# A one-layer streaming encoder: the finale of the last token block of the second feed-forward, turned by diagonal gate matrices behind the last down-projection

## The chip, the cores and the metric

The kernel runs on one core of a Trainium2 chip. The metric is the device time of one execution in microseconds. A run is timed three times and the median counts. The profile is one further execution, with its own time.

Engines are named as in the profile: PE is TensorE (PEld its weight loads), DVE is VectorE, ACT is ScalarE, POOL is GpSimd, SP is SyncE, which here issues every DMA of the program.

## The reference

One layer, cut to what this change touches. It runs for a prompt of 1024 tokens and a sample of 32 tokens, with `D_MODEL` 1024 and `D_FF` 2816; prompt and sample have their own conditioning vector `c`, and so their own gate `g3`.

```python
    x = x + g2[:, None] * rmsnorm(o, gains[3])
    h = adaln_in(x, gains[4], sh3, sc3)
    x = x + FFN_RES * g3[:, None] * rmsnorm(swiglu(h, w2_gate, w2_up, w2_down), gains[5])
    return x, rows
```

`swiglu(h) = (silu(h @ w_gate) * (h @ w_up)) @ w_down`; `rmsnorm` divides each token by the root of its mean square over the 1024 features and multiplies by a gain per feature. All inputs and outputs are float32.

## The kernel before, in words

The 1056 tokens (prompt, then sample) are worked in three blocks `TB`: 0 and 1 have 384 tokens, block 2 has 256 prompt tokens and the 32 of the sample. Activations lie with features on the partitions: a block is `[128, 8, w]`, eight slices `k` of 128 features by `w` tokens. The products of the feed-forward are three float32r matmuls each (`mm3`, L325 to L327).

The second feed-forward is `ffn("h3", ...)`. It goes over 22 slices of `D_FF` in groups of two. For each block, `up` makes gate and up products of both slices (PSUM tiles `gate`, `up`, from the pool of three one-bank buffers, `p1`), ACT and DVE make the gated activation, and `down` multiplies it with the rows of `w_down`: four steps `mp` of 12 matmuls, each into a two-bank tile `dn` (pool `p2`, two buffers), which DVE adds to the accumulator `facc` (L581). In the last group `down(0)` runs behind the first `up` of block 1, `down(1)` behind the first `up` of block 2, and `down(2)` at the very end.

Beside the matmuls runs a list of generators, `side`; `step` advances one of them, `finish` drains the list. Two kinds matter here:

- `tokens_first(tb)` loads the residual stream of a block (`raw`, from `xs`) and turns it by 128x128 transposes on PE (`px`, L1293) to tokens on the partitions; ACT copies the results to `xp` (L1294).
- `finale(tb)` begins in step with the last `down` of its block. `sumsq` squares two slices at a time on ACT (L364), adds them on POOL or DVE (L368, L370) and sums over the features by matmuls with a column of ones (`pss`, L357); `rstd_cols` and `rsqrt` make one reciprocal root per token, 10 small DVE operations in a chain (`rv`, `ry`, `rt`, L334 to L391). Meanwhile every slice of `facc` is multiplied by the gate coefficient of its features (`gcoef`, L1304 on ACT, L1306 on DVE). Then each 128-token tile is transposed in two halves of four slices (`py`, L1313, a `p1` buffer each), and DVE computes `xp = py * rstd + xp` (L1315). One DMA per token tile writes the output (L1318). A block has three token tiles; the third of block 2 is the 32-token sample.

The program is written in this order, and the tile framework's scheduler orders each engine's instructions from it; on the chip each engine works through its list in that order. When the last down-projection was written, `finish` had been called only for block 0, so block 1's finale and block 2's `tokens_first` are drained by the steps of `down(2)` and behind it.

Of the kernel before, what the change touches and what calls it, by code (L numbers as in the profile page):

```python
# [17 lines left out]
KT = D // 128  # L18
# [56 lines left out]
def encoder_step(ctx: ExitStack, tc, x_prompt, x_sample, cache_a_k, cache_a_v, cache_b_k, cache_b_v,  # L75
# [33 lines left out]
    def p2(name, shape=(128, 2, 512)):  # L109
        return ps2.tile(list(shape), F32, name=name, tag="p2")  # L110
# [231 lines left out]
    def token_cols(w):  # L342
        return [(c, min(128, w - c)) for c in range(0, w, 128)]

    def sumsq(src, kts, w, bank, ends, fold=True):


        n = len(kts) // 2
        pss = bank("pss")
        cols = token_cols(w)  # L350
        behind = []

        def add_up(sq, first, last):
            halves = (0,) if fold else (0, 1)
            for q in halves:
                for j, (c0, m) in enumerate(cols):
                    te.matmul(pss[:m, j:j + 1], sq[:, q, c0:c0 + m], ones, start=first and j == 0 and q == 0,  # L357
                              stop=last and q == halves[-1], skip_group_check=True)

        acc, first = None, True  # L360
        for c in range(n):
            k = kts[2 * c]
            sq = h_tile([128, 2, 384], "sq")
            ae.activation(sq[:, :, :w], src[:, k:k + 2, :w], AF.Square)  # L364
            if fold:
                e = SQE[c % len(SQE)]
                e = ve if e == "v" else ge
                e.tensor_tensor(sq[:, 0, :w], sq[:, 0, :w], sq[:, 1, :w], op=OP.add)  # L368
                if acc is not None:
                    e.tensor_tensor(sq[:, 0, :w], sq[:, 0, :w], acc[:, 0, :w], op=OP.add)  # L370
                acc = sq
            if behind:
                add_up(*behind.pop())
            if c in ends or not fold:
                behind.append((sq, first, c == n - 1))
                acc, first = None, False
            yield
        add_up(*behind.pop())
        return pss

# [96 lines left out]
    def step(n):  # L477
        for _ in range(n):
            while side:
                turn[0] += 1  # L480
                i = turn[0] % min(ABREAST, len(side))
                try:
                    next(side[i])
                    break
                except StopIteration:
                    side.pop(i)

    def finish():
        while side:
            step(1)  # L490
# [3 lines left out]
    def begin(key, gen, first=False):  # L494
        side.insert(0 if first else len(side), marked(key, gen))
# [29 lines left out]
    def ffn(key, H, F, wg, wu, wd, per_group, key_out, after, beside=lambda ff, tb: None):  # L525
        late, pre = [], {}
        plan = rounds(*ROUNDS[key])
        begun = set()
        final = {tb: max(i for i, (g, t) in enumerate(plan) if tb in t) for tb in range(3)}

        def load(r, ff):
            pre[r, ff] = (split_cols(wg, ff), split_cols(wu, ff))

        load(0, 0)
        yield
        for r, (gi, blocks) in enumerate(plan):
            grp = GROUPS[gi]
            wgu, wds, gs = {}, {}, {}

            def up(ff, tb):  # L540
                need((key, tb))
                w = TB[tb][1]
                hi, lo = H[tb]
                ps = [p1("gate"), p1("up")]
                for s in range(2):
                    for k in range(KT):
                        mm3(ps[s][:, :w], wgu[ff][s], k, hi[:, k, :], lo[:, k, :], k == 0, k == KT - 1)
                    step(FAST if gi == 0 else PACE)
                sl = s_tile([128, 384], "sl")
                ae.activation(sl[:, :w], ps[0][:, :w], AF.Silu)  # L550
                ve.tensor_tensor(sl[:, :w], sl[:, :w], ps[1][:, :w], op=OP.mult)  # L551
                g = g_tile([128, 2, 384], "gg", F32R)
                ae.activation(g[:, 0, :w], sl[:, :w], AF.Copy)
                ve.tensor_sub(g[:, 1, :w], sl[:, :w], g[:, 0, :w])  # L554
                gs[ff, tb] = g
                beside(ff, tb)
                if late:
                    late.pop()()

            def down(tb, r=r, grp=grp, wds=wds, gs=gs):  # L560
                w = TB[tb][1]
                new = tb not in begun
                begun.add(tb)
                if new:
                    F[tb] = u_tile(tb, "facc", F32)
                if r == final[tb]:
                    if key_out != "y" or tb == 0:
                        finish()
                    own = marked((key_out, tb), after(tb))
                for mp in range(KT // 2):  # L570
                    ps = p2("dn")
                    for s in range(2):
                        for i, ff in enumerate(grp):
                            g = gs[ff, tb]
                            mm3(ps[:, s, :w], wds[ff], 2 * mp + s, g[:, 0, :w], g[:, 1, :w],
                                i == 0, i == len(grp) - 1)
                    o = F[tb][:, 2 * mp:2 * mp + 2, :]
                    if new:
                        ve.tensor_copy(o, ps[:, :, :w])
                    else:  # L580
                        ve.tensor_tensor(o, ps[:, :, :w], o, op=OP.add)  # L581
                    if r == final[tb]:
                        next(own)
                    step(1)
                if r == final[tb]:
                    side.append(own)

            x, y = grp
            if r:
                load(r, x)  # L590
            load(r, y)
            if r == XAT and key == "h1":
                XIN[1] = load_x(1)
            wgu.update({x: pre[r, x], y: pre[r, y]})
            for ff in grp:
                wds[ff] = split_rows(wd, ff)
            for tb in blocks:
                up(x, tb)
                up(y, tb)
                if len(begun) < 2:  # L600
                    down(tb)
                else:
                    late.append(lambda down=down, tb=tb: down(tb))
            if (gi, 2) == (gi, blocks[-1]):
                per_group(gi)
        late.pop()()


# [670 lines left out]

    XP = {}  # L1280

    def tokens_first(tb):

        xp = upool.tile([128, 3, KT, 128], F32, name="xp", tag="u", bufs=6)
        for i, (t, c0, n) in enumerate(token_tiles(tb)):
            xt = XP[tb, i] = xp[:, i]
            xr = rpool.tile([128, KT, 128], F32, name="raw", tag="r")
            dma.dma_start(xr[:, :, :n], xs_dram[2][tb][:, :, c0:c0 + n])
            yield
            for hf in range(2):  # L1290
                pt = p1("px", (128, 4, 128))
                for k in range(4):
                    te.transpose(pt[:n, k, :], xr[:, 4 * hf + k, :n], ident)  # L1293
                ae.activation(xt[:n, 4 * hf:4 * hf + 4], pt[:n], AF.Copy)  # L1294
                yield

    def finale(tb):
        f, w = F3[tb], TB[tb][1]
        pss = yield from sumsq(f, range(KT), w, pc, JF, fold=FF)
        y = rstd_cols(pss, w, 1.0 / D)  # L1300
        for k in range(KT):
            for a, b, st in SEGS[tb]:
                if k % 2:
                    ae.activation(f[:, k, a:b], f[:, k, a:b], AF.Copy, scale=gcoef[:, 2, st, k:k + 1])  # L1304
                else:
                    ve.tensor_scalar(f[:, k, a:b], f[:, k, a:b], gcoef[:, 2, st, k:k + 1], None, op0=OP.mult)  # L1306
            yield
        for i, (t, c0, n) in enumerate(token_tiles(tb)):
            xt = XP[tb, i]
            for k0 in (0, 4):  # L1310
                pt = p1("py", (128, 4, 128))
                for k in range(4):
                    te.transpose(pt[:n, k, :], f[:, k0 + k, c0:c0 + n], ident)  # L1313
                o = xt[:n, k0:k0 + 4]
                ve.scalar_tensor_tensor(o, pt[:n], y[:n, i:i + 1], o, op0=OP.mult, op1=OP.add)  # L1315
                yield
            dst = y_sample[0] if t == SEQ else y_prompt[0, t:t + 128]
            dma.dma_start(dst.rearrange("t (k c) -> t k c", c=128), xt[:n])  # L1318
            yield

    def beside(ff, tb):
        if ff == NF - 1 and tb < 2:
            for t in ((0, 1), (2,))[tb]:
                begin(("xp", t), tokens_first(t))

    for _ in ffn("h3", H3, F3, w2_gate, w2_up, w2_down, lambda gi: None, "y", finale, beside):
        pass
# [28 lines left out]
```

## Time and profile before

| | us |
|---|---|
| median of 3 runs | 2212.97 (2211.99 to 2215.68) |
| time of the profiled execution | 2217.6 |
| its span in the trace | 2215.8 |
| PE busy in it | 2161.6 (98%) |
| DVE busy | 1239.1 (56%) |
| ACT busy | 697.8 (31%) |
| POOL busy | 179.2 (8%) |

The span is what the trace shows from the first to the last instruction; the execution's own time is 1.8 us more. A matmul's record overlaps the next one's, so the distance between the starts of neighbouring matmuls is what one costs; its duration is its latency. Of a float32 matmul that is no transpose the trace holds two records, of a transpose one.

### The profile page before, as it was taken

What the parts mean: (1) busy time and instruction counts of PE and PEld (TensorE: products, weight loads), DVE (VectorE), ACT (ScalarE), POOL (GpSimd) and SP (SyncE); (2) the same over time, 40 slices, a digit from 0 to 9 for tenths busy, and PEclk for the clock granted to TensorE, in tenths of its full rate; (3) what the DMA queues carried; (4) which work ended last, traced back from release to release, by engine and by line L of the source; (5) the groups of instructions that cost most, each with busy time, mean ns of one, the idle gap of its engine ahead of it and who ended that gap; (6) DMA issues with size and microseconds to landing.
All of it is one profiled execution on the core that took longest, in us unless ns stands there. A gap on an engine that the chain in (4) does not pass through costs nothing.

```text
span 2215.8 us, 33976 instructions
## 1 busy us (share of the span) xinstructions
PE 2161.6 (98%) x14012; PEld 2068.6 (93%) x14012; DVE 1239.1 (56%) x2425; ACT 697.8 (31%) x1450; POOL 179.2 (8%) x281
## 2 busy tenths in 40 slices
PE   6999999999999999899999899999999999999998
PEld 4999999999999999799787589999999999999998
DVE  5788667874333497677444865785333333333336
ACT  4411111111121253576444663542111111111133
POOL 1100000000000023001110313220000000000000
PEclk8999999999999999899999899999999999999999
DMA  9253334434122352111112121424211111111122
GB/s 323 93 153 118 111 96 124 143 101 129 39 66 69 101 184 93 38 39 30 50 30 62 46 77 67 134 86 120 66 58 39 57 39 39 58 38 58 39 69 79
DMA packets 200623, 186.03 MB, mean 84 GB/s; under 512 B 7597, under 2 KB 169813, under 8 KB 199317
## 3 DMA queue, kind: packets, MB, share of 16 engines
q1 hardware_dynamic: 200468, 183.87, 27.1%
q8 instruction: 110, 1.80, 0.3%
q14 instruction: 45, 0.36, 0.1%
HBM read 164.12 MB, written 22.86 MB: 84 GB/s over the span
## 4 chain that ended last, share of the span: by engine, by line
PE 90%; DVE 4%; DMA 3%; ACT 1%; issue 1%; POOL 0%; SPq 0%; ACTq 0%; DVEq 0%; POOLq 0%
PE dn L325 7%; PE dn L326 7%; PE dn L327 7%; PE gate L327 7%; PE gate L326 7%; PE up L327 7%; PE up L326 7%; PE gate L325 7%; PE up L325 7%; PE po L713 3%; PE S L752 2%; PE pq L325 2%; PE pq L327 2%; PE pq L326 2%; DMA raw<-in_w_gate_dram 1%; PE pp L776 1%
## 5 line engine op out<-in xcount | busy, mean ns | idle before, releaser
L326 PE MATMUL gate<-h_lo,w 128*128 128x384 f32 (+1 forms) x1056 | 340.2, 322 | 4.0 <-DVE h_lo L446 4.0
L325 PE MATMUL dn<-gg,w 128*128 128x384 f32 (+1 forms) x1056 | 341.4, 325 | 1.1 <-DVE facc L581 1.0
L581 DVE TENSOR_TENSOR facc<-dn,facc 128x768 f32<-128x768 f32 (+1 forms) x240 | 212.9, 889 | 230.2 <-PE dn L327 229.9
L326 PE MATMUL dn<-gg,w 128*128 128x384 f32 (+1 forms) x1056 | 340.6, 323 | 0.6 <-DVE gg L554 0.6
L325 PE MATMUL gate<-h_hi,w 128*128 128x384 f32 (+1 forms) x1056 | 341.0, 323 | 0.0
L327 PE MATMUL gate<-h_hi,w 128*128 128x384 f32 (+1 forms) x1056 | 340.4, 322 | 0.0
L325 PE MATMUL up<-h_hi,w 128*128 128x384 f32 (+1 forms) x1056 | 340.2, 322 | 0.0
L326 PE MATMUL up<-h_lo,w 128*128 128x384 f32 (+1 forms) x1056 | 340.0, 322 | 0.0
L327 PE MATMUL dn<-gg,w 128*128 128x384 f32 (+1 forms) x1056 | 340.0, 322 | 0.0
L327 PE MATMUL up<-h_hi,w 128*128 128x384 f32 (+1 forms) x1056 | 339.9, 322 | 0.0
L304 DVE TENSOR_TENSOR w<-raw,w 128x1024 fp32r<-128x1024 f32 x187 | 231.5, 1246 | 150.5 <-ACT w L303 150.3
L303 ACT ACTIVATE w<-raw 128x1024 fp32r<-128x1024 f32 x187 | 195.7, 1056 | 266.1 <-PE dn L327 103.5
L550 ACT ACTIVATE sl<-gate 128x384 f32<-128x384 f32 (+1 forms) x132 | 60.9, 462 | 563.9 <-PE gate L327 560.9
L551 DVE TENSOR_TENSOR sl<-sl,up 128x384 f32<-128x384 f32 (+1 forms) x132 | 68.5, 519 | 292.1 <-PE up L327 286.1
L326 PEld LDWEIGHTS gate<-h_lo,w 128*128 128x128 f32 x1056 | 198.6, 188 | 4.6 <-DVE h_lo L446 4.6
L325 PEld LDWEIGHTS dn<-gg,w 128*128 128x128 f32 x1056 | 199.2, 189 | 1.6 <-DVE facc L581 1.2
L326 PEld LDWEIGHTS dn<-gg,w 128*128 128x128 f32 x1056 | 199.2, 189 | 1.0 <-DVE gg L554 0.9
L327 PEld LDWEIGHTS dn<-gg,w 128*128 128x128 f32 x1056 | 199.1, 189 | 0.0
L325 PEld LDWEIGHTS gate<-h_hi,w 128*128 128x128 f32 x1056 | 198.7, 188 | 0.1
L327 PEld LDWEIGHTS gate<-h_hi,w 128*128 128x128 f32 x1056 | 198.7, 188 | 0.0
L327 PEld LDWEIGHTS up<-h_hi,w 128*128 128x128 f32 x1056 | 198.7, 188 | 0.0
L325 PEld LDWEIGHTS up<-h_hi,w 128*128 128x128 f32 x1056 | 198.5, 188 | 0.0
(224 smaller groups left out, 3367.4 us busy)
## 6 DMA issues: line engine op xcount, KB each, us to landing
raw<-in_w_mod_dram SPq DMA_DIRECT2D x56, 512.0 KB, 4.0
raw<-in_w_gate_dram SPq DMA_DIRECT2D x54, 512.0 KB, 4.0
raw<-in_w_up_dram SPq DMA_DIRECT2D x54, 512.0 KB, 4.7
raw<-in_w_down_dram SPq DMA_DIRECT2D x54, 512.0 KB, 4.5
raw<-in_w_in_dram SPq DMA_DIRECT2D x18, 512.0 KB, 4.3
wm<-in_w_mod_dram SPq DMA_DIRECT2D x8, 1024.0 KB, 7.4
raw<-in_w_out_dram SPq DMA_DIRECT2D x13, 512.0 KB, 4.5
xr<-xs SPq DMA_DIRECT2D x16, 384.0 KB, 3.5
```

The source lines that it names most:

```text
L303: ae.activation(w[:, 0], r, AF.Copy)
L304: ve.tensor_sub(w[:, 1], r, w[:, 0])
L325: te.matmul(ps, w[:, 0, k], hi, start=start, stop=False)
L326: te.matmul(ps, w[:, 0, k], lo, start=False, stop=False)
L327: te.matmul(ps, w[:, 1, k], hi, start=False, stop=stop)
L550: ae.activation(sl[:, :w], ps[0][:, :w], AF.Silu)
L551: ve.tensor_tensor(sl[:, :w], sl[:, :w], ps[1][:, :w], op=OP.mult)
L581: ve.tensor_tensor(o, ps[:, :, :w], o, op=OP.add)
L713: te.matmul(po[64 * h:64 * h + 64, :n], vsl(j, h, kn), PT(h, j, kn), start=j == 0, stop=j == nt - 1)
L752: te.matmul(S[:, c:ce], self.T[:, h, :], KQ[:, 0, 128 * k0 + c:128 * k0 + ce], start=True, stop=True)
L776: te.transpose(pp[:, j - j0, :], P[:, 128 * j:128 * j + 128], ident)
```

## The change

The gate multiplication of `facc` is gone. In its place two diagonal tiles `DG` (one for the prompt's gate, one for the sample's) are made once on POOL from the identity and `gcoef`, 16 operations (L1315 of the changed kernel). The transposes of the finale become float32 matmuls of a 128x128 slice of `facc` with the diagonal (`turned`, `py` at L1320), which turn and scale at once. This holds for all three blocks.

All generators are drained before the last down-projection, which takes no steps of its own. The finale of block 2 is a function of its own, `last_finale`: its `raw` tiles are loaded early (`load_xr`); `px` and `py` of block 2 are written behind the last down-projection; the first two token tiles get two-bank tiles `py2` from `p2`. The sum of squares closes with three groups of `pss` instead of one. DVE combines the two prompt tiles (L1371); for the sample ACT scales (`yz`, L1368) and POOL adds (L1369). Each half of a token tile is written by its own DMA.

```diff
@@ sumsq
-            halves = (0,) if fold else (0, 1)
+            halves = (0,) if fold and not (apart and last) else (0, 1)
...
-            if fold:
+            if fold and not (apart and c == n - 1):
@@ ffn
-                    step(1)
+                    if key_out != "y" or tb < 2:
+                        step(1)
...
+        if key_out == "y":
+            finish()
         late.pop()()
@@ finales
+    def load_xr(tb, i):
+        t, c0, n = token_tiles(tb)[i]
+        xr = XR[tb, i] = rpool.tile([128, KT, 128], F32, name="raw", tag="r")
+        dma.dma_start(xr[:, :, :n], xs_dram[2][tb][:, :, c0:c0 + n])
...
+    def gates_diagonal():
+        for st in range(2):
+            DG.append(wpool.tile([128, KT, 128], F32, name="dg", tag="w"))
+            for k in range(KT):
+                ge.tensor_scalar(DG[st][:, k, :], ident, gcoef[:, 2, st, k:k + 1], None, op0=OP.mult)
+                if k % 4 == 3:
+                    yield
+
+    def turned(pt, f, k, c0, n, t):
+        te.matmul(pt, f[:, k, c0:c0 + n], DG[1 if t == SEQ else 0][:, k, :], start=True, stop=True)
...
     def finale(tb):
         f, w = F3[tb], TB[tb][1]
-        pss = yield from sumsq(f, range(KT), w, pc, JF, fold=FF)
+        last = tb == 2
+        pss = yield from sumsq(f, range(KT), w, pc, (2, 3) if last else JF, fold=FF, apart=last)
         y = rstd_cols(pss, w, 1.0 / D)
-        for k in range(KT):
-            for a, b, st in SEGS[tb]:
-                if k % 2:
-                    ae.activation(f[:, k, a:b], f[:, k, a:b], AF.Copy, scale=gcoef[:, 2, st, k:k + 1])
-                else:
-                    ve.tensor_scalar(f[:, k, a:b], f[:, k, a:b], gcoef[:, 2, st, k:k + 1], None, op0=OP.mult)
-            yield
+        if last:
+            yield from last_finale(f, y)
+            return
...
-                    te.transpose(pt[:n, k, :], f[:, k0 + k, c0:c0 + n], ident)
+                    turned(pt[:n, k, :], f, k0 + k, c0, n, t)
...
+    def last_finale(f, y):
+        pts = {}
+        back = tokens_first(2, loaded=True)
+        tiles_ = token_tiles(2)
+        for i, (t, c0, n) in enumerate(tiles_):
+            for k0 in (0, 4):
+                next(back)
+                if i < 2:
+                    if k0 == 0:
+                        pts[i] = p2("py2", (128, 2, 4, 128))
+                    pt = pts[i][:, k0 // 4]
+                else:
+                    pt = p1("py", (128, 4, 128))
+                for k in range(4):
+                    turned(pt[:n, k, :], f, k0 + k, c0, n, t)
+                pts[i, k0] = pt
+        for i, k0 in ((2, 0), (0, 0), (2, 4), (0, 4), (1, 0), (1, 4)):
+            t, c0, n = tiles_[i]
+            pt, o, yc = pts[i, k0][:n], XP[2, i][:n, k0:k0 + 4], y[:n, i:i + 1]
+            if i == 2:
+                z = h_tile([128, 4, 128], "yz")
+                ae.activation(z[:n], pt, AF.Copy, scale=yc)
+                ge.tensor_tensor(o, z[:n], o, op=OP.add)
+            else:
+                ve.scalar_tensor_tensor(o, pt, yc, o, op0=OP.mult, op1=OP.add)
+            put(t, n, k0, o)
+        yield
```

Up to the last group of the second feed-forward every engine's list is the same in both programs. Three places show what moves. First, PE behind the last matmul of the last down-projection (`dn`, not shown), to the end of the program, before:

```order
L1293 MATMUL px<-ident,raw 32x128 x4
L1313 MATMUL py<-ident,facc 128x128 x28
L357 MATMUL pss<-ones,sq 128x1 x2
L357 MATMUL pss<-ones,sq 32x1
L1313 MATMUL py<-ident,facc 128x128 x12
L1313 MATMUL py<-ident,facc 32x128 x8
```

and in the changed program, from the same matmul up to the last `pss` (behind them stand 6 more `py` of 128x128, 8 of 32x128, and 12 `px`):

```order
L1320 MATMUL py_20378<-dg,facc 128x128 x4
L1304 MATMUL px<-ident,raw 128x128 x8
L1320 MATMUL py_20378<-dg,facc 128x128 x2
L1304 MATMUL px<-ident,raw 128x128 x4
L357 MATMUL pss<-ones,sq 128x1 x2
L357 MATMUL pss<-ones,sq 32x1
L1320 MATMUL py_20378<-dg,facc 128x128 x2
L1320 MATMUL py_20399<-dg,facc 128x128 x2
L357 MATMUL pss<-ones,sq 128x1 x2
L357 MATMUL pss<-ones,sq 32x1
L357 MATMUL pss<-ones,sq 128x1 x2
L357 MATMUL pss<-ones,sq 32x1
```

All 24 `py` of block 1 have left this place, 20 `px` of block 2 have come to it, and 10 turns and 12 `px` now stand ahead of the last `pss`. Second, PE between the third and the fourth step of the last down-projection in the changed program:

```order
L325 MATMUL dn<-gg,w 128x288
L326 MATMUL dn<-gg,w 128x288
L327 MATMUL dn<-gg,w 128x288
L1320 MATMUL py<-dg,facc 128x128 x12
L325 MATMUL dn<-gg,w 128x288
L326 MATMUL dn<-gg,w 128x288
L327 MATMUL dn<-gg,w 128x288
```

These are the last 12 turns of block 1; its other 12 stand further up, between gate, up and down matmuls. Third, DVE from the last step of block 1's reciprocal root to the first operation of block 2's (`rv`), in the changed program:

```order
L338 SCALAR_TENSOR_TENSOR ry<-rt,ry 128x3
L1341 SCALAR_TENSOR_TENSOR xp<-py,ry,xp 128x512 x3
L581 TENSOR_TENSOR facc<-dn,facc 128x576 x2
L1341 SCALAR_TENSOR_TENSOR xp<-py,ry,xp 128x512 x2
L368 TENSOR_TENSOR sq<-sq 128x288
L1341 SCALAR_TENSOR_TENSOR xp<-py,ry,xp 128x512
L370 TENSOR_TENSOR sq<-sq 128x288
L581 TENSOR_TENSOR facc<-dn,facc 128x576
L388 TENSOR_SCALAR rv<-pss 128x2
```

Before, the six combining operations of block 1 (L1315, now L1341) stood behind the last L581, among the additions of the squares; now they stand ahead of it.

## Rows read from the trace of the kernel before

**Rows 1.** busy time by stretch (us from the span's start; busy us, instructions; PEclk is granted clock)

```profile
core 0: us, PE busy (x) PEld busy (x) DVE busy (x) ACT busy (x) POOL busy (x), PEclk, DMA share, GB/s
...
2160.00:2180.00 20.00, 20.00 (x135) 19.94 (x134) 8.98 (x22) 4.63 (x8) 1.40 (x2) 1.00 0.03 4
...
2199.00:2216.00 17.00, 8.76 (x58) 6.47 (x55) 13.14 (x34) 3.18 (x7) 0.00 (x0) 0.77 0.42 162
```

**Rows 2.** PE in order of time from the last `dn` (start us, us, what, [idle before])

```profile
2198.61 0.30 PE L327 MATMUL dn<-gg,w 128*128 128x288 f32 x1
2198.74 0.60 PE L1293 MATMUL px<-ident,raw 128*32 128x128 f32 x4
2199.18 1.04 PE L1313 MATMUL py<-ident,facc 128*128 128x128 f32 x8
...
2205.11 0.69 PE L357 MATMUL pss<-ones,sq 128*128 128x1 f32 x6
...
2209.26 2.79 PE L1313 MATMUL py<-ident,facc 128*128 128x128 f32 x12 [2.30 <-DVE xp L1315]
```

**Rows 3.** DVE in order of time in the same stretch

```profile
2198.41 1.41 DVE L581 TENSOR_TENSOR facc<-dn,facc 128x576 f32<-128x576 f32 x2
...
2204.47 0.46 DVE L370 TENSOR_TENSOR sq<-sq 128x288 f32<-128x288 f32 x1
2204.84 1.41 DVE L1315 SCALAR_TENSOR_TENSOR xp<-py,ry,xp 128x512 f32<-128x512 f32 x2
2206.16 0.16 DVE L388 TENSOR_SCALAR rv<-pss 128x2 f32<-128x2 f32 x1
...
2208.17 0.16 DVE L338 SCALAR_TENSOR_TENSOR ry<-rt,ry 128x3 f32<-128x3 f32 x1
2208.36 4.47 DVE L1315 SCALAR_TENSOR_TENSOR xp<-py,ry,xp 128x512 f32<-128x512 f32 x6
```

**Rows 4.** PE in order of time: four transposes among matmuls of 384 columns

```profile
2174.32 0.60 PE L1313 MATMUL py<-ident,facc 128*128 128x128 f32 x4
2174.67 0.42 PE L325 MATMUL dn<-gg,w 128*128 128x384 f32 x1
2174.93 0.34 PE L326 MATMUL dn<-gg,w 128*128 128x384 f32 x1
2175.11 0.34 PE L327 MATMUL dn<-gg,w 128*128 128x384 f32 x1
```

**Rows 5.** PE: three float32 matmuls 128x128 (`pr`, six records)

```profile
1370.86 0.83 PE L405 MATMUL pr<-ident,ry 128*128 128x128 f32 x6
1371.45 0.42 PE L327 MATMUL wo<-o_hi,w 128*128 128x384 f32 x1
1371.70 0.34 PE L325 MATMUL wo<-o_hi,w 128*128 128x384 f32 x1
```

**Rows 6.** PE: the same three matmuls elsewhere

```profile
1485.45 0.94 PE L405 MATMUL pr<-ident,ry 128*128 128x128 f32 x6
1486.32 0.44 PE L325 MATMUL dn<-gg,w 128*128 128x384 f32 x1
1486.60 0.34 PE L326 MATMUL dn<-gg,w 128*128 128x384 f32 x1
```

**Rows 7.** PE: nine float32 matmuls with weights of 64 columns (18 records)

```profile
1122.90 1.31 PE L713 MATMUL po<-PT,vt 128*64 128x128 f32 x18
1124.13 0.44 PE L327 MATMUL pq<-h_hi,w 128*128 128x384 f32 x1
1124.41 0.34 PE L325 MATMUL pq<-h_hi,w 128*128 128x384 f32 x1
```

**Rows 8.** groups of POOL by form (count | busy us, mean ns | idle before)

```profile
L368 POOL TENSOR_TENSOR sq<-sq 128x384 f32<-128x384 f32 x32 | 35.3, 1116 | 1422.0 <-ACT sq L364 1400.0 <-PE S L752 13.3 <-DVE w L304 5.0
...
L467 POOL TENSOR_TENSOR facc<-facc,xr 128x576 f32<-128x576 f32 x2 | 2.8, 1433 | 13.7 <-DVE facc L464 13.7
```

**Rows 9.** ACT in order of time behind the last `dn`: a copy of 32x512 from PSUM

```profile
2200.54 0.57 ACT L1294 ACTIVATE xp<-px 32x512 f32<-32x512 f32 x1
```

More of the change, by code (lines that the diff above doesn't have):

```diff
@@ L343, in token_cols, with sumsq @@
         return [(c, min(128, w - c)) for c in range(0, w, 128)]
-    def sumsq(src, kts, w, bank, ends, fold=True):
+    def sumsq(src, kts, w, bank, ends, fold=True, apart=False):
         n = len(kts) // 2
@@ L1280, in encoder_step, with tokens_first @@
     XP = {}
-    def tokens_first(tb):
+    XR = {}
+    def load_xr(tb, i):
+        t, c0, n = token_tiles(tb)[i]
+        xr = XR[tb, i] = rpool.tile([128, KT, 128], F32, name="raw", tag="r")
+        dma.dma_start(xr[:, :, :n], xs_dram[2][tb][:, :, c0:c0 + n])
+    def tokens_first(tb, loaded=False):
         xp = upool.tile([128, 3, KT, 128], F32, name="xp", tag="u", bufs=6)
@@ L1286, in tokens_first @@
             xt = XP[tb, i] = xp[:, i]
-            xr = rpool.tile([128, KT, 128], F32, name="raw", tag="r")
-            dma.dma_start(xr[:, :, :n], xs_dram[2][tb][:, :, c0:c0 + n])
-            yield
+            if not loaded:
+                load_xr(tb, i)
+                yield
+            xr = XR.pop((tb, i))
             for hf in range(2):
@@ L1295, in tokens_first, with put @@
                 yield
+    DG = []
+    def gates_diagonal():
[7 more added lines that the diff above has]
+        te.matmul(pt, f[:, k, c0:c0 + n], DG[1 if t == SEQ else 0][:, k, :], start=True, stop=True)
+    def put(t, n, k0, o):
+        dst = y_sample[0] if t == SEQ else y_prompt[0, t:t + 128]
+        dma.dma_start(dst.rearrange("t (k c) -> t k c", c=128)[:, k0:k0 + o.shape[1]], o)
     def finale(tb):
         f, w = F3[tb], TB[tb][1]
-        pss = yield from sumsq(f, range(KT), w, pc, JF, fold=FF)
+        last = tb == 2
+        pss = yield from sumsq(f, range(KT), w, pc, (2, 3) if last else JF, fold=FF, apart=last)
         y = rstd_cols(pss, w, 1.0 / D)
-        for k in range(KT):
-            for a, b, st in SEGS[tb]:
-                if k % 2:
-                    ae.activation(f[:, k, a:b], f[:, k, a:b], AF.Copy, scale=gcoef[:, 2, st, k:k + 1])
-                else:
-                    ve.tensor_scalar(f[:, k, a:b], f[:, k, a:b], gcoef[:, 2, st, k:k + 1], None, op0=OP.mult)
-            yield
+        if last:
+            yield from last_finale(f, y)
+            return
         for i, (t, c0, n) in enumerate(token_tiles(tb)):
@@ L1316, in finale @@
                 yield
-            dst = y_sample[0] if t == SEQ else y_prompt[0, t:t + 128]
-            dma.dma_start(dst.rearrange("t (k c) -> t k c", c=128), xt[:n])
+            put(t, n, 0, xt[:n])
             yield
+    def last_finale(f, y):
[24 more added lines that the diff above has]
+            put(t, n, k0, o)
+        yield
     def beside(ff, tb):
         if ff == NF - 1 and tb < 2:
-            for t in ((0, 1), (2,))[tb]:
-                begin(("xp", t), tokens_first(t))
+            if tb == 0:
+                begin("diagonal", gates_diagonal(), first=True)
+                for t in range(2):
+                    begin(("xp", t), tokens_first(t))
+            else:
+                for i in range(3):
+                    load_xr(2, i)
     for _ in ffn("h3", H3, F3, w2_gate, w2_up, w2_down, lambda gi: None, "y", finale, beside):
```

## Prediction

> **What bounds the kernel now.** The view of busy time by stretch comes first: from 2160 to 2180 us PE is busy 20.00 of 20 us at full clock, from 2199 on 8.76 of 17 at a mean clock of 0.77 [rows 1]. So up to the last down-projection whatever is added to PE's list lengthens the run and whatever another engine is spared shortens nothing. Behind it PE waits, and a chain sets the end. The views in order of time show it. PE is free of the last `dn` at 2198.74 (where the next instruction starts); behind it come the 48 turns `py` of blocks 1 and 2, with `pss` among them at 2205.11 [rows 2]. DVE, after the last addition to `facc` (2198.41 plus 1.41, two of them), has block 1's combining operations still ahead of it; the last addition of squares starts at 2204.47, `rv` at 2206.16, and the root is done at 2208.17 + 0.16 = 2208.33 [rows 3]. Six combining operations then take 4.47 us to 2212.83 [rows 3], and the last DMA and the end of the program the 2.97 up to 2215.8. From PE's freedom to the end it is 17.06 us.
>
> **The price of a turn.** This decides the case. The change turns by 72 float32 matmuls of 128x128 (8 of them with 32 columns of weights) in place of 72 transposes. Four transposes among down matmuls take 2174.93 - 2174.32 = 0.61 us with the one `dn` behind them, whose own distance is 0.18: 0.43, or 0.109 each [rows 4]. The nearest rows for the new kind are `pr`: weights 128x128 and 128 moving columns, float32, two records a matmul. Three of them take 1371.70 - 1370.86 = 0.84 with one matmul behind, less 0.17: 0.67, 0.226 a matmul (0.223 by the division, 0.226 at 0.113 a record) [rows 5]. That is twice a transpose. The same three take 1.15 - 0.17 = 0.98, or 0.326 each, in another place [rows 6]: the upper end. With weights of 64 columns, nine take 1.51 - 0.17 = 1.34, or 0.149 each [rows 7]: the lower end. I take 0.226, since shape and type are the turn's.
>
> The Trainium skill, page "FP8 and Floating Point Precision", section "TensorE Precision Notes", says that true float32 takes four passes through the array. If every pass cost what a transpose does, a turn would be an estimated 0.44 us, and the sum below 12 us more; the trace does not agree, its float32 matmul of that shape takes 0.226 [rows 5].
>
> **PE up to the last `dn`.** Block 0's 24 turns stay ahead of it: 24 x (0.226 - 0.109) = +2.8. Block 1's 24 come ahead of it, from a place where PE was waiting: 24 x 0.226 = +5.4. Of block 2's transposes `px`, 20 leave: -20 x 0.109 = -2.2. Sum +6.0: PE is free at 2204.8 instead of 2198.74. I add no stall. Block 0's first eight turns only fill buffers; the ninth needs a combining operation, which follows a root of 2.2 us, while PE has 24 `up` matmuls of 0.17 (4.2 us) to do. Block 1's last 12 turns need its root and three combining operations of 0.75; by the same prices the first is done about 0.9 us before PE arrives, the others earlier still against their turns.
>
> **What is spared and costs nothing, or helps nothing.** The gate multiplications (L1304, L1306) of blocks 0 and 1 lay on ACT and DVE beside a full PE; they buy nothing there. The 16 diagonal operations on POOL replace nothing; POOL is next to idle and a 128x384 addition there takes 1.1 us [rows 8], so 16 of 128x128 take some 6 us, at most 18 if each were as dear as that whole addition, beside some 80 gate and up matmuls of 0.17 and a step of down on PE (16 us); without that cover block 0's squares on POOL, and so its root and its ninth turn, would come later. SP gets three more output DMAs and moves the loads of block 2's `raw` ahead; nothing queued behind them is wanted sooner.
>
> **The chain behind the last `dn`,** counted from PE's freedom (P). PE goes through its list: 4 turns (0.9), 8 `px` (0.9), 2 turns (0.45), 4 `px` (0.45), a `pss` group (0.7: 3 x 0.226), 4 turns (0.9), two more `pss` groups (1.35): P + 5.6. The squares are ready long before: DVE's last addition to `facc` ends near P + 1.15, ACT squares 0.7 more. So it is PE's list, not the squares, that `pss` waits for. `rv` starts about 0.2 later and the root takes what it took (2206.16 to 2208.33): P + 7.95, against 9.6 before. DVE's four combining operations at 0.7 to 0.75: P + 10.8. The sample's way is longer: behind `pss` PE has 6 turns, 12 `px` and 8 turns of 32 columns (0.6 for four, at the 0.149 of the narrow rows [rows 7]) to P + 9.5; ACT scales the second half from P + 9.75 to 10.3 (0.57 for such a copy [rows 9]); POOL adds 512 columns in 1.3 us, between its 1.12 for 384 and 1.43 for 576 [rows 8]; the first addition ends at 10.55, the second at 11.85. Then 2.97 for the DMA and the end: P + 14.8. That is 2.2 us less than 17.06.
>
> **Sum.** +6.0 - 2.2 = +3.8 us: the span goes from 2215.8 to 2219.6, the execution from 2217.6 to 2221.4. The profiled execution lies 4.6 above the median, so the forecast for the median is 2212.97 + 3.8 = **2216.8 us**, 0.17% more. What a measurement here can tell from no change is 0.2%, or 4.4 us (2208.5 to 2217.4).
>
> **Rivals.** 58 turns lie on the path (48 ahead of P, 10 ahead of the last `pss`), so each 0.01 us of a turn's price is worth 0.58 us, and the change breaks even at 0.226 - 3.8 / 58 = 0.160.
>
> 1. *A turn is slow,* 0.326 as in [rows 6]: 58 x 0.1 = +5.8 more, 2222.6, clearly slower. For: the same matmul does so in several places, at the same clock. Against: the other half of the places. It decides from a price of 0.236 on, where the loss passes 4.4 us. 12%.
> 2. *A turn is cheap,* 0.149 or less: 58 x 0.077 = -4.5, 2212.3, no change; at a transpose's 0.109 it would be 2210.0, and with a sample's way that ends with DVE's another 1 us less, near the bound of faster. For: nine matmuls of 64 columns run at that price. Against: the weights here have 128. 17%, a third of it beyond 0.2%.
> 3. *A turn runs the array four times,* each as dear as a transpose: 4 x 0.109 = 0.44, and 58 x 0.21 = +12.2, 2229.0. For: no row. Against: [rows 5], half that price at the same shape. 3%. This is the rule of the page named above.
> 4. *The clock falls under the last turns.* Before, PE fell from 0.109 to 2.79 / 12 = 0.23 a transpose behind its wait at the end [rows 2], half the clock. If it falls right behind the last `pss`, the 3.9 us of PE work there become 7.8, and the second half of the sample, no longer held up by the first on POOL, ends at P + 15.5 instead of 11.85: +3.6, 2220.4. For: the mean of 0.77 over that stretch [rows 1]. Against: PE has no wait between the last `dn` and its last turn now. 5%.
>
> **How the numbers follow.** The forecast has 63%, with its own range 2214.0 to 2219.5 (a matmul price off by 0.02, POOL off by 0.5, a median off by 1.5); it crosses the bound of slower in two cases of five. Slower: 0.26 from it, 0.12, 0.03 and 0.05 from rivals 1, 3 and 4: 0.46. Faster: 0.05, out of rival 2. The rest, 0.49, is within 0.2%. The range that holds 8 in 10 reaches from the cheap turns to the slow ones without the four passes: 2211.5 to 2222.5.
>
> **What would show it.** Right: two records of about 0.113 a turn; the last `dn` some 6 us later; no idle on PE from block 0's turns to the last `pss`; `pss` 5 to 6 us behind the last `dn`, with its squares done 3 us before; POOL's second addition as the last work, a microsecond behind DVE's. Wrong: a turn at one record or at four; a wait of PE on a combining operation in the last group; a `pss` that waits for squares; a clock below full between the last `dn` and the last turn; an end set by DVE.

## Result and profile after

| | before | changed |
|---|---|---|
| first measurement, median (lowest to highest), 5 runs each | 2212.97 (2211.99 to 2215.68) | 2222.94 (2215.61 to 2224.37) |
| ratio, 95% interval | | 1.0037 [1.0019, 1.0055] |
| the same kernel again, 12 runs, beside 35 of before | 2215.02 | 2220.91 |
| ratio, 95% interval | | 1.0026 [1.0017, 1.0036] |
| profiled execution: its time, its span | 2217.6, 2215.8 | 2215.61, 2213.8 |

The median of before that the earlier section gives for 3 runs is that of these 5. The change makes the kernel slower. By the larger measurement it is 0.26%, 5.9 us (3.8 to 8.0 by the interval); the first, of five runs, says 10 us (4.2 to 12.2). The forecast was 3.8 us more. The profiled execution of the changed kernel is the fastest of its five, so its span cannot be set against that of before as a whole. It has to be cut, and the cut shows why.

Busy time by stretch, 840 to 1480 us, in the kernel before and then in the changed kernel (columns as in [rows 1]; the lists of instructions are the same here, but the window is cut by time):

```profile
840.00:1480.00 640.00, 614.34 (x4246) 540.31 (x4245) 418.84 (x1131) 343.48 (x883) 128.05 (x229) 0.96 0.21 63
```

```profile
840.00:1480.00 640.00, 613.91 (x4290) 541.24 (x4289) 423.20 (x1143) 344.39 (x884) 129.63 (x229) 0.98 0.21 64
```

In these 640 us PE gets through more of the same list in the changed kernel (4290 records against 4246), at a mean granted clock of 0.98 against 0.96. In the second profile of each kernel (first two experiments below) it is 0.97 for both. So the span falls into three pieces: the front, up to the last group of the second feed-forward; from there to P, where PE is free of the last `dn`; and the tail, from P to the end. The front is read up to the first 384-column `dn` of block 0's last down-projection, less 0.109 us for each `px` that stands ahead of that `dn` in the last group.

| execution | front | to P | tail | to P and tail |
|---|---|---|---|---|
| before | 2143.12 | 55.62 | 17.06 | 72.68 |
| before, profiled again | 2144.19 | 55.62 | 16.59 | 72.21 |
| changed | 2136.19 | 62.03 | 15.58 | 77.61 |
| changed, profiled again | 2142.46 | 62.02 | 15.62 | 77.64 |

The front differs by 6.3 us between two executions of the changed kernel, and by 8.0 over the four; the mean granted clock of the whole execution is 0.984 in both of before, 0.989 and 0.987 in those of the changed kernel, and the shorter fronts go with the higher clock. The part that the change touches repeats to 0.5 us: +4.9 by the first profile of each kernel, +5.4 by the second. That is where the loss is read from here on.

PE in order of time in the changed kernel, from block 1's last turns, which now stand in the last down-projection, to the end of the list (columns as in [rows 2], to which these answer):

```profile
2193.97 2.84 PE L1320 MATMUL py<-dg,facc 128*128 128x128 f32 x24
2196.56 0.38 PE L325 MATMUL dn<-gg,w 128*128 128x288 f32 x1
2196.78 0.29 PE L326 MATMUL dn<-gg,w 128*128 128x288 f32 x1
...
2198.09 0.29 PE L327 MATMUL dn<-gg,w 128*128 128x288 f32 x1
2198.22 1.05 PE L1320 MATMUL py<-dg,facc 128*128 128x128 f32 x8
2199.11 1.04 PE L1304 MATMUL px<-ident,raw 128*128 128x128 f32 x8
...
2200.87 0.66 PE L357 MATMUL pss<-ones,sq 128*128 128x1 f32 x6
2201.45 1.16 PE L1320 MATMUL py<-dg,facc 128*128 128x128 f32 x8
2202.45 1.34 PE L357 MATMUL pss<-ones,sq 128*128 128x1 f32 x12
...
2206.13 1.06 PE L1320 MATMUL py<-dg,facc 128*32 128x128 f32 x8
2207.12 0.61 PE L1304 MATMUL px<-ident,raw 128*32 128x128 f32 x4
2207.66 1.06 PE L1320 MATMUL py<-dg,facc 128*32 128x128 f32 x8
```

No row from P on has a wait. Twelve turns and one `dn` behind them take 2196.78 - 2193.97 = 2.81 us; less 0.13 for the `dn` that is 0.223 a turn. DVE in the same stretch, which answers to [rows 3]:

```profile
2198.88 0.74 DVE L581 TENSOR_TENSOR facc<-dn,facc 128x576 f32<-128x576 f32 x1
2203.83 0.16 DVE L388 TENSOR_SCALAR rv<-pss 128x2 f32<-128x2 f32 x1 [4.20 <-PE pss L357]
...
2205.85 0.16 DVE L338 SCALAR_TENSOR_TENSOR ry<-rt,ry 128x3 f32<-128x3 f32 x1
2206.13 2.73 DVE L1371 SCALAR_TENSOR_TENSOR xp<-py,ry,xp 128x512 f32<-128x512 f32 x4
```

DVE waits 4.20 us for `pss`, has the root at P + 7.8 and is done at P + 10.6. What ended last is the sample's way. The chain that ended last, its final pieces in order of time:

```profile
2206.20 1.00 PE py L1320 x8
2207.21 0.03 ACTq L1368
2207.23 0.05 issue
2207.28 0.69 ACT yz L1368
2207.97 0.07 issue
2208.03 1.26 POOL xp L1369
2209.29 0.27 issue
2209.56 1.29 POOLq L1411
```

POOL's second addition (2209.60 plus 1.25) ends at P + 12.63, two microseconds behind DVE, and 2.95 us later the span ends. The 0.27 before its last piece, which the chain calls issue, is a wait in the view in order of time, for ACT's second scaling (`yz`, which ends at 2209.52) and not for POOL's own first addition (2209.29):

```profile
2208.84 0.68 ACT L1368 ACTIVATE yz<-py,ry 32x512 f32<-32x512 f32 x1 [0.41 <-PE py L1320]
2209.60 1.25 POOL L1369 TENSOR_TENSOR xp<-yz,xp 32x512 f32<-32x512 f32 x1 [0.31 <-ACT yz L1368]
```

### The profile page after: what moved, and what is told of

The parts are those of the page before. It is cut to its first block, busy times and chain, and to the rows that moved or that the text cites. A ratio compares the mean times of both kernels' runs of the same rounds, so it can differ in the third digit from the quotient of the medians.

```text
span 2213.8 us, 34151 instructions
## 1 busy us (share of the span) xinstructions
PE 2161.7 (98%) x14096; PEld 2071.1 (94%) x14096; DVE 1228.6 (55%) x2405; ACT 691.7 (31%) x1436; POOL 192.6 (9%) x299
## 4 chain that ended last, share of the span: by engine, by line
PE 88%; DVE 5%; DMA 4%; ACT 1%; issue 1%; POOL 0%; SPq 0%; POOLq 0%; ACTq 0%; DVEq 0%
PE up L327 7%; PE up L326 7%; PE up L325 7%; PE dn L325 7%; PE gate L327 7%; PE dn L326 7%; PE gate L326 7%; PE dn L327 7%; PE gate L325 7%; PE po L716 3%; PE S L755 2%; PE pq L325 2%; PE pq L327 2%; PE pq L326 2%; DMA raw<-in_w_gate_dram 1%; PE pp L779 1%
## 5 line engine op out<-in xcount | busy, mean ns | idle before, releaser
L581 DVE TENSOR_TENSOR facc<-dn,facc 128x768 f32<-128x768 f32 (+1 forms) x240 | 212.7, 888 | 238.4 <-PE dn L327 238.4
L327 PEld LDWEIGHTS up<-h_hi,w 128*128 128x128 f32 x1056 | 198.7, 188 | 0.0
L326 PEld LDWEIGHTS up<-h_lo,w 128*128 128x128 f32 x1056 | 198.5, 188 | 0.0
```

The lines of the kernel that those rows point to most:

```text
L326: te.matmul(ps, w[:, 0, k], lo, start=False, stop=False)
L327: te.matmul(ps, w[:, 1, k], hi, start=False, stop=stop)
```

## Experiments

**Theory.** The loss is PE's: 48 turns that cost two transposes each stand on PE's list up to P, where PE is full, and 24 of them, with nothing to hide them, come from behind P. What the change wins behind P is the early root, and the late sample gives part of it back. **Rivals:** the difference is the front's spread and not the change; the new order costs it, not the price of a turn; the sample's way over three engines costs it. In the expectations T is this theory, C a rival that puts the loss elsewhere, and e5 and e6 are experiments 4 and 5.

**1 and 2. Both kernels again.** No edit. The changed kernel:

> The changed kernel once more, unaltered. Theory T (the extra PE work of the turns decides: the last dn comes 6 us later, the tail is 2 us shorter): 4 to 6 us slower than before in the median, and a trace in which the stretch from the first px to the end is 5 us longer than before's, whatever the stretch ahead of it does. Rival C (the changed kernel is 10 us slower because of a mechanism in or behind the last group that the first profiled execution escaped, such as half the clock under the last turns): 9 to 10 us slower, and the trace shows a stretch from the first px to the end that is 9 us or more longer than before's.

The kernel before, as a kernel of its own beside it:

> The kernel before once more, unaltered, as a second trace of it. Both theories: within 2 us of before in the median. Its stretch ahead of the first px says how much executions of one program differ there: T expects several us of difference to the first trace at different granted clocks between 850 and 1500 us, C expects under 1 us.

Measured: changed 2220.91, ratio 1.0026 [1.0017, 1.0036]; before 2216.07, ratio 1.0008 [0.9997, 1.0019] to itself. The loss is real, since its interval keeps clear of 1, and some 4 of the first 10 us were not the change's. Before against itself differs by 0.08%, with an interval that takes in 1: about what such a comparison can tell. The cut by stretches is in the table above: the changed part is 4.9 and 5.4 us longer, as T has it, and not 9. The fronts of the two profiles of before differ by 1.1 us only, where T expected several; the wide difference is that between the two of the changed kernel.

**3. Plain turns.** The turns become transposes again; the gate multiplication is left out.

```diff
-        te.matmul(pt, f[:, k, c0:c0 + n], DG[1 if t == SEQ else 0][:, k, :], start=True, stop=True)
+        te.transpose(pt, f[:, k, c0:c0 + n], ident)
```

> The changed kernel with its 72 turns as transposes by the identity; the gate coefficient is left out of the result. T: a turn costs 0.109 instead of 0.226 us, 48 of them ahead of the end of the last dn and 10 ahead of the last pss: 6 to 7 us faster than the changed kernel, so 1 to 3 us faster than before. C (the cause lies in the order of work or in the clock, not in the price of a turn): within 2 us of the changed kernel.

Measured: 2215.75, ratio 1.0000 [0.9990, 1.0009]; to P 55.26, tail 16.16, together 71.42. By the stretches that is 6.2 us less than the changed kernel, as expected; by the medians (2220.91 and 2215.75) 5.2, and nothing against before. The loss is gone, so it hangs on the price of the turns. The edit did more than it should: with cheaper turns the scheduler left 12 of block 1's behind the last `dn`. PE behind the last `dn` in this run:

```profile
2197.94 3.22 PE L1320 MATMUL py<-ident,facc 128*128 128x128 f32 x28
2201.00 1.94 PE L1304 MATMUL px<-ident,raw 128*128 128x128 f32 x16
2202.78 2.05 PE L357 MATMUL pss<-ones,sq 128*128 128x1 f32 x18
```

To P the difference of 6.77 to the changed kernel is accounted for: 36 turns cheaper by 0.223 - 0.109 = 0.114 are 4.1, 12 turns gone from there at 0.223 are 2.7. Without any price for the gate the new structure is 0.8 to 1.3 us better than before (71.42 against 72.21 and 72.68), so the order itself loses nothing.

**4. Diagonals in the last block alone.** Blocks 0 and 1 get back their gate multiplication on ACT and DVE and their transposes.

```diff
+        for k in range(KT):
+            for a, b, st in SEGS[tb]:
+                if k % 2:
+                    ae.activation(f[:, k, a:b], f[:, k, a:b], AF.Copy, scale=gcoef[:, 2, st, k:k + 1])
+                else:
+                    ve.tensor_scalar(f[:, k, a:b], f[:, k, a:b], gcoef[:, 2, st, k:k + 1], None, op0=OP.mult)
+            yield
...
-                    turned(pt[:n, k, :], f, k0 + k, c0, n, t)
+                    te.transpose(pt[:n, k, :], f[:, k0 + k, c0:c0 + n], ident)
```

> The changed kernel, but blocks 0 and 1 keep the gate multiplication on ACT and DVE and their transposes; only block 2 is turned by the diagonals. T: the last dn ends 5.6 us earlier than in the changed kernel (24 x 0.117 for block 0, 24 x 0.117 for block 1), the tail is longer by about 1 us because 4 more turns stand ahead of the last pss: 4 to 5 us faster than the changed kernel, within 2 us of before. C: within 2 us of the changed kernel.

Measured: 2215.38, ratio 1.0002 [0.9992, 1.0013]; to P 56.58, tail 15.80, together 72.38. To P it wins 5.45 us on the changed kernel, and 48 turns by 0.114 are 5.5. Here the result is computed in full, with the gate in blocks 0 and 1 on engines that have time. This is the clean form of experiment 3: the whole loss lies in the turns of blocks 0 and 1. The tail was expected 1 us longer than the changed kernel's and is 0.2 longer. The root is late as said (DVE's four combining operations start at P + 8.8, not 7.9), but the sample's way ends last here too, at P + 12.6 as in the changed kernel: there the root had that much to spare.

**5. The sums first.** With the diagonals as in the change, the `pss` groups are put straight behind 12 `px`, and all turns of block 2 behind them, tile 1 last.

```diff
...
+        with tc.issue_after(closing[0].ins):
+            turn_tile(0)
+            for _ in range(3):
+                next(back)
+            turn_tile(2)
+        with tc.issue_after(turn_end[0].ins):
+            turn_tile(1)
...
-        for i, k0 in ((2, 0), (0, 0), (2, 4), (0, 4), (1, 0), (1, 4)):
+        for i, k0 in ((0, 0), (2, 0), (0, 4), (2, 4), (1, 0), (1, 4)):
```

> The changed kernel with PE's list behind the last dn put in another order: 12 px, then the three pss groups, then the turns of tile 0, the rest of px, the turns of the sample, the turns of tile 1. If pss waits for PE's own list and not for the squares, the last pss starts about 2 us behind the last dn's neighbour in the list instead of 4.2, PE waits about 0.5 us for the squares, the root is ready at 6.2 instead of 7.8, and the tail is 14.6 to 14.8 instead of 15.6 us, since PE's 10.2 us of work there is then the bound; the run is about 1 us faster than the changed kernel, within the noise of a median. If the squares were the limit, the last pss starts no earlier and the tail keeps its 15.6.

Measured: 2221.64, ratio 1.0026 [1.0015, 1.0036]; to P 62.11, tail 16.04, which is 0.4 longer than the changed kernel's, where 14.6 to 14.8 was expected. The root came early and nothing came of it. DVE at the end of this run (P is 2203.66):

```profile
2209.51 0.16 DVE L338 SCALAR_TENSOR_TENSOR ry<-rt,ry 128x3 f32<-128x3 f32 x1
2209.82 1.41 DVE L1387 SCALAR_TENSOR_TENSOR xp<-py,ry,xp 128x512 f32<-128x512 f32 x2
2214.70 1.41 DVE L1387 SCALAR_TENSOR_TENSOR xp<-py,ry,xp 128x512 f32<-128x512 f32 x2 [3.47 <-PE py L1323]
```

The root is done at P + 6.0, 1.8 us before the changed kernel's; then DVE stands 3.47 us until PE has tile 1's turns, PE's last work at P + 11. DVE's last operation ends at P + 12.45 (2214.70 plus 1.41), no later than the last work of the changed kernel (P + 12.63); but the span ends 3.59 us behind it, not 2.95. What is written last here is half a prompt tile, 256 KB, not half the sample, 64 KB (from issue to landing 2.1 us, the median in experiment 8, against 1.6 here). Whatever PE does last must be cheap to combine: the tail ends with the later of two things, the root and its combining operations, or PE's list and what hangs on its last item. Behind both comes the last output.

**6. The sample on DVE.** ACT's scaling and POOL's addition go; DVE combines all six, the sample last (`i == 3` never holds).

```diff
-        for i, k0 in ((2, 0), (0, 0), (2, 4), (0, 4), (1, 0), (1, 4)):
+        for i, k0 in ((0, 0), (0, 4), (1, 0), (1, 4), (2, 0), (2, 4)):
...
-            if i == 2:
+            if i == 3:
```

> The changed kernel with the sample's two halves combined by DVE behind the prompt's four, instead of ACT and POOL. If the way over ACT and POOL ends last by itself (12.6 us behind the last dn, DVE idle from 10.6), the tail becomes 15.0 (10.6 + 2 x 0.7 + 2.95) instead of 15.6. If sharing pays, the tail is longer than 15.6.

Measured: 2221.88, ratio 1.0030 [1.0019, 1.0041]; to P 62.00, tail 14.92, 0.7 shorter than the changed kernel's, and so 0.7 less in the stretches, too little for the medians. DVE's last row:

```profile
2213.09 4.03 DVE L1371 SCALAR_TENSOR_TENSOR xp<-py,ry,xp 128x512 f32<-128x512 f32 x6
```

Six operations in a row without a wait; the span ends 2.98 us behind them. So the sharing over three engines cost 0.7 us against one engine: the two additions on POOL (1.26 and 1.25) and their wait for ACT are longer than two more operations on DVE at 0.66.

**7. No diagonals at all.** The order of experiment 5, with gate multiplication on ACT and DVE and transposes in all three blocks. The edit against experiment 5:

```diff
...
+                    ve.tensor_scalar(f[:, k, a:b], f[:, k, a:b], gcoef[:, 2, st, k:k + 1], None, op0=OP.mult)
...
-                    turn_end[:] = [turned(pt[:n, k, :], f, k0 + k, c0, n, t)]
+                    turn_end[:] = [te.transpose(pt[:n, k, :], f[:, k0 + k, c0:c0 + n], ident)]
...
```

> The order of e6 without any diagonal: all blocks keep the gate multiplication on ACT and DVE and plain transposes. T: the stretch from the first px to the last dn as in e5 (56.6 us, 5.4 less than the changed kernel), the last pss starts about 2 us behind it, and PE's list behind it is 2.7 us shorter than in e6; tail 13.0 to 13.6 us. Sum 69.6 to 70.2 against 72.2 to 72.7 before and 77.6 with the change: 2 to 3 us faster than before, 7 to 8 faster than the change. If the diagonals bought the tail something that the order can't (the gate multiplication in the way of the squares on ACT and DVE), the tail is 15 us or more.

Measured: 2216.09, ratio 1.0004 [0.9995, 1.0012]; to P 56.12 and a tail of 16.73. A miss: the tail was expected 3 us shorter. DVE and PE behind P (2199.87):

```profile
2198.69 2.05 DVE L1351 SCALAR_TENSOR_TENSOR xp<-py,ry,xp 128x512 f32<-128x512 f32 x3
2200.66 0.49 DVE L1339 TENSOR_SCALAR facc<-facc,gcoef 128x256 f32<-128x256 f32 x2
2201.07 0.74 DVE L584 TENSOR_TENSOR facc<-dn,facc 128x576 f32<-128x576 f32 x1
...
2202.10 0.49 DVE L1339 TENSOR_SCALAR facc<-facc,gcoef 128x256 f32<-128x256 f32 x2
2202.51 0.45 DVE L373 TENSOR_TENSOR sq<-sq 128x288 f32<-128x288 f32 x1
```

```profile
2203.11 2.10 PE L359 MATMUL pss<-ones,sq 128*128 128x1 f32 x18 [1.65 <-DVE sq L373]
2205.14 1.77 PE L1376 MATMUL py<-ident,facc 128*128 128x128 f32 x8
2206.71 2.50 PE L1307 MATMUL px<-ident,raw 128*128 128x128 f32 x12
```

Two things went wrong at once. The last addition to `facc` stands on DVE behind three combining operations of block 1 and two gate multiplications and starts at P + 1.2, so the squares are late and PE waits 1.65 us. And behind that wait a transpose takes (2206.71 - 2205.14) / 8 = 0.196 us, not 0.109. The last work, POOL's, ends at P + 13.1, and 3.64 us lie behind it. The gate multiplication is part of the lateness: two pairs of it stand ahead of the last addition of squares, 2201.07 - 2200.66 and 2202.51 - 2202.10 = 0.41 each, 0.8 of the 1.65. That the diagonals of the last block take it off DVE and ACT is their use there; no run has this order with diagonals in block 2 alone, so what they are worth as a whole is not shown.

**8. What each half is good for.** Diagonals in block 2 alone, as in experiment 4; PE's list written out, with six turns of tile 0, 12 `px` and two turns in the time in which the squares become ready; the sample last, on DVE.

```diff
...
+        turn_tile(0)
+        with tc.issue_after(closing[0].ins):
+            next(back)
+            turn_tile(1)
+        with tc.issue_after(turn_end[0].ins):
+            for _ in range(2):
+                next(back)
+            turn_tile(2)
+        for i, k0 in ((0, 0), (0, 4), (1, 0), (1, 4), (2, 0), (2, 4)):
...
```

> Blocks 0 and 1 of the last feed-forward keep their gate multiplication on ACT and DVE and their plain transposes, as in the kernel before; only block 2 turns through the diagonals. PE's list behind the last down-projection is written out: six turns of tile 0 and twelve px, the last two turns of tile 0, then the three pss groups, then tile 1 and the sample; DVE combines all six results in the order tile 0, tile 1, sample. My theory (the loss of the change sits on PE ahead of the last down-projection, its gain behind it is the early root): the stretch from block 2's down-projection to PE's freedom P stays at 56.6 us as in the run with diagonals in block 2 alone, pss starts at P + 3.1 to 3.3 (6 turns 1.35, 12 px 1.3, 2 turns 0.45; squares ready by then), root at P + 7.6, six combining operations 4.0, the last DMA and the end 3.0: a tail of 14.6, against 15.8 in that run and 16.6 to 17.1 before. Sum of the two stretches 71.2 against 72.2 to 72.7 before, so 1.0 to 1.5 us less; ratio 0.9990 to 0.9995. Rival 1 (the sample is late, its narrow turns at 0.25 each): PE ends at P + 10.7, the sample's first operation on DVE waits 0.3 to 0.5 and the tail is 15.0. Rival 2 (the squares come late as in the run without diagonals, behind block 1's combining operations on DVE, and the clock halves): pss starts at P + 3.5 or later with PE idle before it, transposes behind it at 0.2 instead of 0.11, tail 16 or more, no better than before.

Measured: 2213.77, ratio 0.9992 [0.9983, 1.0001]; to P 56.27, tail 14.44, together 70.71: 1.5 to 2.0 us less than before in the stretches, the best of all. The median agrees (-1.8 us by the ratio), but its interval just takes in no change: that this order is faster rests on one profile of it against two of before. PE and DVE behind P (2198.86):

```profile
2198.86 1.50 PE L1323 MATMUL py<-dg,facc 128*128 128x128 f32 x12
2200.20 1.47 PE L1307 MATMUL px<-ident,raw 128*128 128x128 f32 x12
2201.51 0.61 PE L1323 MATMUL py<-dg,facc 128*128 128x128 f32 x4
2201.96 2.03 PE L359 MATMUL pss<-ones,sq 128*128 128x1 f32 x18
```

```profile
2204.03 0.16 DVE L391 TENSOR_SCALAR rv<-pss 128x2 f32<-128x2 f32 x1 [3.30 <-PE pss L359]
...
2206.32 4.03 DVE L1395 SCALAR_TENSOR_TENSOR xp<-py,ry,xp 128x512 f32<-128x512 f32 x6
```

`pss` starts at P + 3.1 with no wait before it, the root serves DVE from P + 7.5, six combining operations end at P + 11.5. Neither rival of this run came: the sample is not late, and the clock does not fall.

| run | ratio to before | to P | tail | together |
|---|---|---|---|---|
| before (two profiles) | | 55.62, 55.62 | 17.06, 16.59 | 72.68, 72.21 |
| changed (two profiles) | 1.0026 [1.0017, 1.0036] | 62.03, 62.02 | 15.58, 15.62 | 77.61, 77.64 |
| 3 plain turns, no gate | 1.0000 [0.9990, 1.0009] | 55.26 | 16.16 | 71.42 |
| 4 diagonals in the last block | 1.0002 [0.9992, 1.0013] | 56.58 | 15.80 | 72.38 |
| 5 sums first | 1.0026 [1.0015, 1.0036] | 62.11 | 16.04 | 78.15 |
| 6 sample on DVE | 1.0030 [1.0019, 1.0041] | 62.00 | 14.92 | 76.92 |
| 7 no diagonals | 1.0004 [0.9995, 1.0012] | 56.12 | 16.73 | 72.85 |
| 8 both halves | 0.9992 [0.9983, 1.0001] | 56.27 | 14.44 | 70.71 |

From the last combining operation to the end of the span it is 2.94 to 2.99 us in both profiles of before, both of the changed kernel, and experiments 6 and 8, but 3.72, 3.22, 3.59 and 3.64 in experiments 3, 4, 5 and 7. Between these two groups up to 0.8 us of a tail is that stretch alone; beyond the reason given in experiment 5 the cause is open.

## Why the prediction was right, and where it was off

The mechanism held; the sum was 1.1 to 1.6 us too low by the stretches (+3.8 against +4.9 and +5.4), and 2.1 by the larger measurement, whose interval begins at +3.8. The likeliest case named was a loss too small to be told from nothing; what came is one just over that bound, with 0.46 on it. The first median, 2222.94, lies 0.4 above the range of 8 in 10, and far above the forecast's own, which ends 6.5 us above before; +5.9 lies inside both. Its excess over the stretches is of the size by which the front differs between executions, but one of its executions alone is cut by stretches, so where it sits in the others is not shown.

- **The price of a turn** [rows 5]: 0.226 forecast, 0.223 measured in place. Right, and it decided the case. Rivals 1 and 2 fall with it. Rival 3 falls too: the Trainium skill, page "FP8 and Floating Point Precision", section "TensorE Precision Notes", gives true float32 four passes, which at a transpose's 0.109 each would be 0.44; the runs show two records of 0.112. What falls with it is the price put on a pass, not the count: a float32r matmul of 384 columns takes 0.18 us [rows 4], an estimated 0.06 for 128 of them, and four times that is 0.24.
- **PE up to P:** +6.0 forecast, +6.4 measured. The three terms come to 5.9 at the measured price. "I add no stall" failed: PE waits 0.29 us in block 0's part for ACT to copy a `px` tile out, a wait that before does not have there and the second profile repeats. The row of the changed kernel:

```profile
2149.94 0.63 PE L1304 MATMUL px<-ident,raw 128*128 128x128 f32 x4 [0.29 <-ACT xp L1305]
```

  The other 0.2 are not traced to a row.
- **The chain to the root:** `pss` forecast to end at P + 5.6, with `rv` 0.2 behind; `rv` starts at P + 5.61. Root P + 7.95 against 7.8, DVE's end P + 10.8 against 10.6. The squares were ready 2 us ahead (ACT's last square ends at 2200.40, the last `pss` groups begin at 2202.45), so PE's list was what `pss` waited for, as said; the forecast had put the margin at 3.
- **The sample's way:** the mis-sized term, and a wait that was named wrongly. Four narrow turns were taken at 0.6 from rows with 64 columns of weights [rows 7]; they took 2207.12 - 2206.13 = 0.99. Twice 0.39 is 0.8 of the 1.0 by which PE's list ended late (2207.66 plus 1.06, P + 10.5 against 9.5). ACT's second scaling (`yz`) followed it, and ended at P + 11.3 against 10.3. The forecast had POOL's second addition held up by POOL's first; the trace has it wait for that scaling. It ended at P + 12.63 against 11.85, and so the tail came out 0.8 longer (15.58 against 14.8). With an end set by PE's last turn all 24 turns of block 2 were on the path, and not only the 10 ahead of the last `pss` that the forecast's 58 count.
- **The baseline:** the tail of before was 17.06 in the profile read and 16.59 in the next. Half a microsecond of the gain was the luck of that execution: the six combining operations at its end took 4.47 us and in the next profile 4.03, while PE's last 12 transposes took 2.79 and 1.84.
- **The clock** (rival 4) stayed at 1.00 under the turns; from 2204 to 2209 us, in the changed kernel:

```profile
2204.00:2209.00 5.00, 4.72 (x40) 3.77 (x39) 4.39 (x15) 2.50 (x5) 0.97 (x1) 1.00 0.25 94
```

- **POOL's diagonals** took 9.4 us (16 of 0.60), not 6, and cost nothing, as said: they ran beside a full PE from 2122 us on.

## What to carry to other kernels

Fold a scaling into a matmul only where the engine that scaled was late: here the same diagonals cost 5.5 us in two blocks whose scaling was hidden beside a full PE. In the one block behind which PE waits they cost nothing that shows (experiment 4, 72.38 together against 72.21 and 72.68); that they gain there by themselves is not shown, since experiment 8 changed the order and the sample's engine too. A tail ends with the later of two chains, the reduction with its consumers and PE's list with the consumer of its last item, and then with the last output; shortening one alone (experiment 5) gave nothing, and in experiment 8, where both chains end within the six combining operations, the tail is the shortest. Where executions differ by more in a part that the change leaves alone than the change is worth, cut the span there and compare the rest.

## What the runs showed of the hardware

- A float32 matmul with 32 columns of weights and 128 moving columns is no cheaper than one with 128: eight records of either kind last 1.06 and 1.05 us, and with the change to `px` behind them the narrow group takes 0.99 from start to start, the wide one at P 0.89.
- The granted clock of the front (840 to 1480 us) was 0.96, 0.97 and 0.98 in executions of the same list of instructions. The one at 0.98 has a front 6 to 8 us shorter than the other three; between 0.96 and 0.97 the front does not follow (2143.12 at 0.96, 2144.19 and 2142.46 at 0.97).
- In experiment 7 the clock fell behind a wait of 1.65 us, in the middle of a busy tail, though not at once: the 18 `pss` records right behind the wait took 2.03 us from start to start, little more than the 1.96 in experiment 8. Busy time by stretch there, and then in experiment 5, where PE waited 0.38 us at the same place and the clock held:

```profile
2203.20:2206.60 3.40, 3.40 (x26) 3.31 (x27) 1.32 (x10) 0.21 (x1) 0.00 (x0) 0.82 0.00 0
2206.60:2211.00 4.40, 4.36 (x30) 3.55 (x28) 2.10 (x8) 2.91 (x5) 0.52 (x1) 0.75 0.32 119
```

```profile
2203.00:2209.00 6.00, 5.62 (x51) 5.46 (x50) 3.32 (x13) 2.14 (x4) 0.05 (x1) 1.00 0.37 150
2209.00:2214.00 5.00, 5.00 (x45) 4.51 (x45) 1.98 (x6) 2.90 (x5) 1.42 (x2) 1.00 0.30 106
```

- An addition of 128x288 on DVE (L368) took 0.98 us instead of 0.46 [rows 3] while POOL ran its own addition of squares (2196.81 plus 0.81). The second profile has 0.97 at the same place, and experiment 8, where POOL had ended by then, 0.45. No run tries it by itself. Here it hid behind PE's list.
